# The end of a decoder layer: last block by column halves, last root on GpSimd, last scalings in one tile

## The chip, the cores and the metric

The kernel runs on one core of one Trainium2 chip. The metric is the device time of one execution in microseconds; the figure of a kernel is the median over several executions. The engines are named as in the profile: PE is TensorE (PEld its weight loads), DVE is VectorE, ACT is ScalarE, POOL is GpSimd, SP is SyncE, which issues most of the DMA transfers.

## What is computed

One layer of a decoder over 512 tokens of width 1024, all in float32. Only the last part matters here: the channel mixer's down projection, its residual add, and the final norm.

```python
        u2 = _rmsnorm(h, norm2_g[l])
        z = _causal_dwconv(u2 @ w_ffn_up[l], ffn_dw_w[l], ffn_dw_b[l])
        h = h + (jax.nn.silu(z[..., :FFN_DIM]) * z[..., FFN_DIM:]) @ w_ffn_down[l]
    return _rmsnorm(h, final_g)

def _rmsnorm(x, g):
    xf = x.astype(jnp.float32)
    y = xf * lax.rsqrt(jnp.mean(xf * xf, axis=-1, keepdims=True) + EPS)
    return (y * g.astype(jnp.float32)).astype(x.dtype)
```

## The kernel before

Tokens lie in four row tiles t = 0 to 3 of P = 128 tokens, the width of 1024 in two halves n = 0, 1 of T = 512 columns. The residual is held in SBUF as eight tiles `hres[t, n]` of 128x512. Each float32 operand is split into a high and a low part, and one product of such operands is three matmuls (`mm3`, lines 288 to 294: low x high, high x low, high x high). A PSUM tile is 128x512 float32.

The two big square projections (output and down projection) run through `seven` (line 816), which forms a two-by-two block product from seven block products instead of eight. The steps go in the order of `STEPS`: a11, a12, s1, n2, s4, n3, a22. Each step has two blocks, i = 0 and 1, and a block is four operand pairs by three matmuls, twelve matmuls of 512 columns into one PSUM tile (line 844). After a block, line 859 adds or subtracts the PSUM tile into one `hres` tile on VectorE; `into` says which. The step a12 completes `hres` of row tiles 0 and 1, n = 0; s4 completes row tiles 0 and 1, n = 1; n3 completes row tiles 2 and 3, n = 1; a22, the last step, completes row tiles 2 and 3, n = 0. So the last block of the program is (a22, i = 1), which completes row tile 3.

The down projection is done in three groups of channels; in the last of them `complete` is `last_complete` (line 995) and `at` is `last_at` (line 1001). When a half of a row tile is complete, `Finish.half` squares it on ScalarE with a running sum (`square_sum`, line 875: an activation and the reading of its accumulator) and multiplies it by the gain on VectorE (line 976), in place for the first half found, into a `tmp` tile for the second. When both halves are there, `total_rstd` adds the two sums and EPS on VectorE (line 880), and `rsqrt` raises the total to the power -1/2 on GpSimd (line 340). `Finish.store` scales both halves by that root: the half found last on ScalarE (line 985), the other on ScalarE (line 990) for row tiles 0 and 1, on VectorE (line 988) for 2 and 3; each half goes out by its own DMA of 256 KB that SyncE issues (lines 986 and 991).

Weights of the last step come in through the two buffers `kept` (lines 184 to 204): they are split into high and low parts by ScalarE (line 231) and VectorE (line 232) one step ahead. The tile framework orders the instructions of each engine when the program is built, by when it expects them to be ready, so the order on an engine can differ from that of the text; waits between engines and on buffers are put in by it as well.

Of the kernel before, what the change touches and what calls it, by code (L numbers as in the profile page):

```python
# [10 lines left out]
F32 = mybir.dt.float32  # L11
# [3 lines left out]
AF = mybir.ActivationFunctionType  # L15
ALU = mybir.AluOpType

P = 128
D = 1024
T = 512  # L20
NT = T // P
# [10 lines left out]
EPS = 1e-6  # L32
# [32 lines left out]
def trunk_layer(ctx: ExitStack, tc: tile.TileContext, a: dict, out: bass.AP):  # L65
    nc = tc.nc
# [5 lines left out]
    def scoped(name, bufs, side="left"):  # L72
        scope = ExitStack()
        return scope, scope.enter_context(tc.tile_pool(name=name, bufs=bufs, side=side))
# [14 lines left out]
    def nm(s):  # L89
        return f"{s}_{next(names)}"  # L90

    def heap(dt=F32):
        return hp.tile([P, T], dt, tag="h", name=nm("h"))

    def tmp(n=T):
        return tp.tile([P, n], F32, tag="tmp", name=nm("tmp"), bufs=5)
# [7 lines left out]
    def small(n, tag):  # L104
        return tp.tile([P, n], F32, tag=tag, name=nm(tag), bufs=4)

    def mm_bank():
        return ps.tile([P, T], F32, tag="mm", name=nm("mm"), bufs=5)

    def ax_bank():  # L110
        return ps.tile([P, T], F32, tag="ax", name=nm("ax"), bufs=3)
# [7 lines left out]
    mhalf = cp.tile([P, NT], F32, name="mhalf")  # L119
# [36 lines left out]
    kept = {}  # L156
# [97 lines left out]
    def prefetch(n):  # L254

        while len(ready) < min(used[0] + n, len(order)):
            split_weight()

    def weight(name, j, ahead=LOOK):
        assert order[used[0]] == (name, j)  # L260
        prefetch(1)
        used[0] += 1
        prefetch(ahead)
        fill(RATE)
        return ready[used[0] - 1]
# [6 lines left out]
    def fill(n):  # L272
        room[0] += n
        while chains and room[0] > 0:
            room[1] += 1
            chain = chains[room[1] % min(2, len(chains))]
            share, work = chain.pop(0)
            room[0] -= share
            with tc.issue_after(pace[0].ins):
                work()  # L280
            if not chain:
                chains.remove(chain)
                if not chains and after:
                    chains.append(after.pop()())
        if not chains:
            room[0] = 0.0
# [51 lines left out]
    def rsqrt(v, n):  # L338
        r = small(n, "rstd")
        nc.gpsimd.tensor_tensor(r, v, mhalf[:, :n], ALU.pow)  # L340
        return r
# [6 lines left out]
    def junk(n):  # L348
        return tp.tile([P, n], BF16, tag="junk", name=nm("junk"), bufs=1)
# [109 lines left out]
    for k in range(KT):  # L459
# [4 lines left out]
        c = heap()  # L464
# [95 lines left out]
    rows = slice(32, 32 + RANK)  # L560
# [9 lines left out]
    rows = slice(96, 96 + RANK)  # L570
# [184 lines left out]
    late_scope, late = scoped("late", 1, "right")  # L755


    part = [None] * KT
# [15 lines left out]
    H = T // 2  # L774
# [18 lines left out]
    for p, q in O_PAIRS:  # L793
# [6 lines left out]
        s1, n2, n3, s4 = e1[:, :H], e1[:, H:], e2[:, :H], e2[:, H:]  # L800
# [12 lines left out]
    ctx.push(res_scope)  # L813


    def seven(name, pairs, acts, complete, at=lambda step, i: None):

        bank = {"x": [mm_bank(), mm_bank()], "y": [mm_bank(), mm_bank()], "z": [ax_bank(), ax_bank()]}
        of = {"a11": "x", "n2": "x", "n3": "x", "a22": "x", "s1": "y", "s4": "y", "a12": "z"}

        into = {
            "a11": (0, 0, ALU.add, False),
            "a12": (0, 0, ALU.add, True),
            "s1": (1, 1, ALU.add, False),
            "n2": (0, 1, ALU.subtract, False),
            "s4": (0, 1, ALU.add, True),  # L830
            "n3": (1, 1, ALU.subtract, True),
            "a22": (1, 0, ALU.add, True),
        }

        def products(step, i, parts):
            acc = bank[of[step]][i]
            opens = step in ("a11", "s1", "a12")
            for d, w in parts:
                for j, pair in enumerate(acts[2 * d : 2 * d + 2]):
                    ah, al = (x[:, i * P : (i + 1) * P] for x in pair[step])  # L840
                    c = slice(j * T, (j + 1) * T)

                    read = 2 * d + j == len(acts) - 1
                    mm3(acc, (ah, al), (w[0][:, c], w[1][:, c]), opens and d == 0 and j == 0, read, not opens)

        steps = list(STEPS)
        while steps:
            step, d = steps.pop(0)
            parts = [(d, weight(name, (pairs, step, d)))]
            if steps and steps[0] == (step, 1):  # L850
                steps.pop(0)
                parts.append((1, weight(name, (pairs, step, 1))))
            for i in range(2):
                products(step, i, parts)
                if parts[-1][0] == 1:
                    at(step, i)
                    half, n, op, whole = into[step]
                    t = 2 * half + i
                    nc.vector.tensor_tensor(hres[t, n], hres[t, n], bank[of[step]][i], op)  # L859
                    if whole:  # L860
                        complete(t, n)


    gain2 = load_gain("norm2_g")
    hres = {}
# [6 lines left out]
    def square_sum(key, src, n):  # L872
        if key not in ss2:
            ss2[key] = small(2, "ss2")
        nc.scalar.activation(junk(T), src, AF.Square, scale=1.0 / 32.0, accum_out=ss2[key][:, n : n + 1])

    def total_rstd(key):
        v = small(1, "var")
        s = ss2[key]
        nc.vector.scalar_tensor_tensor(v, s[:, 0:1], EPS, s[:, 1:2], ALU.add, ALU.add)  # L880
        return rsqrt(v, 1)
# [7 lines left out]

    normed, roots = {}, {}  # L890

    def o_complete(t, n):
        square_sum(("n2", t), hres[t, n], n)
        if n == (0 if t > 1 else 1):
            roots[t] = total_rstd(("n2", t))
            if t > 1:
                normed[t] = norm2(t, roots[t])
# [19 lines left out]
    ffn_scope, fp = scoped("ffn", 1)  # L917
    gain3 = load_gain("final_g")
# [31 lines left out]
    def second_of_pair(i, accs, w, acts):  # L950
# [11 lines left out]
        acts["s1"], acts["n2"], acts["s4"] = y(0), y(1), y(2)  # L962
        return acts

    class Finish:


        def __init__(self, t):
            self.t, self.found = t, []

        def half(self, n):
            hn = hres[self.t, n]
            square_sum(("n3", self.t), hn, len(self.found))
            g = gain3[:, n * T : (n + 1) * T]
            y = tmp() if self.found else hn
            nc.vector.tensor_tensor(y, hn, g, ALU.mult)
            self.found.append((n, y))

        def scale(self):
            self.r = total_rstd(("n3", self.t))  # L980

        def store(self, late):
            rows = slice(self.t * P, (self.t + 1) * P)
            (m, x), (n, y) = self.found
            nc.scalar.activation(y, y, AF.Copy, scale=self.r)
            nc.sync.dma_start(out[rows, n * T : (n + 1) * T], y)
            if late:
                nc.vector.tensor_scalar(x, x, self.r, None, ALU.mult)
            else:
                nc.scalar.activation(x, x, AF.Copy, scale=self.r)  # L990
            nc.sync.dma_start(out[rows, m * T : (m + 1) * T], x)

    ends = [Finish(t) for t in range(NT)]

    def last_complete(t, n):
        ends[t].half(n)
        if len(ends[t].found) == 2 and t > 1:
            ends[t].scale()
            ends[t].store(True)

    def last_at(step, i):

        if (step, i) == ("a22", 0):
            for end in ends[:2]:
                end.scale()
            for end in ends[:2]:
                end.store(False)

    for gi, pairs in enumerate(GROUPS):
        acts = []  # L1010
        early = {}
        if gi == 0:

            ws = [weight("w_up", j, 0) for i in pairs[0] for j in (i, FT + i)]
            accs = [mm_bank() for _ in ws]
            for lo in (0, T // 2):
                for j, (w, acc) in enumerate(zip(ws, accs)):
                    col_tile(w, acts2, acc, lo, lo + T // 2)
                    if lo == 0 and j > 1:
                        to_channels(normed[j], u2, j)  # L1020
            early = {pairs[0][0]: accs[:2], pairs[0][1]: accs[2:]}

        def both(i):
            return early.get(i) or [col_tile(weight("w_up", i), acts2), col_tile(weight("w_up", FT + i), acts2)]

        for p, q in pairs:
            w, found = first_of_pair(p, both(p))
            acts.append(second_of_pair(q, both(q), w, found))
        if gi < len(GROUPS) - 1:
            seven("w_down", pairs, acts, lambda t, n: None)  # L1030
        else:
            seven("w_down", pairs, acts, last_complete, last_at)
    ffn_scope.close()


# [87 lines left out]
```

## Time and profile before

| what | value |
|---|---|
| median of 3 executions | 849.79 us (849.37 to 850.01) |
| the profiled execution: its time | 850.15 us |
| the profiled execution: its span | 848.4 us |
| mean granted clock of TensorE | 0.998 |
| TensorE busy | 835.3 us, 98% |
| matmuls of 128x512 (line 292 in the large groups) | 384 ns mean, pipelined |

The span is the time from the first to the last instruction in the trace; the execution's own time has 1.75 us more around it. Rows of the time line give the start in us from the span's start, the duration in us, the engine, the line, the operation, out<-in with the program's names and shapes, and in square brackets how long the engine was idle before and what released it. Rows of groups give the busy time in us and the mean of one in ns, then the idle time before. Matmuls overlap in the pipeline: each row of a matmul of 512 columns says 0.39 us, and they start about 0.23 us apart.

### The profile page before, as it was taken

The numbers are of one execution on the slowest core, as the hardware profiler recorded it, in microseconds if no ns is written. First come the engines' busy times: TensorE is split into PE (matmuls) and PEld (weight loads), VectorE is DVE, ScalarE is ACT, GpSimd is POOL, SyncE is SP. The second block draws the span as 40 slices with busy tenths as digits, with TensorE's granted clock in tenths as the row PEclk, the third lists the DMA queues.
The fourth block names the chain that finished last, engine by engine and source line by source line (L and its number), as shares of the span: only waits on it lengthen the run. The fifth ranks groups of instructions, "written<-read, shape, count | busy, mean of one in ns | idle before, by whom it ended". The sixth has DMA issues, their size and how long they took to land.

```text
span 848.4 us, 9947 instructions
## 1 busy us (share of the span) xinstructions
PE 835.3 (98%) x3814; PEld 691.0 (81%) x3814; DVE 646.1 (76%) x913; ACT 383.3 (45%) x531; POOL 42.6 (5%) x60
## 2 busy tenths in 40 slices
PE   8999999999999999999999999999999999999996
PEld 6888888888888888788888788888888888888885
DVE  5479879999998788744688749778767777677795
ACT  5433336535443422449444526444334443444454
POOL 1000000000100100000001100000100010000011
PEclk9999999999999999999999999999999999999999
DMA  8223232222222322222338533225732238222462
GB/s 288 94 100 104 95 107 81 97 96 81 94 75 75 124 100 99 75 99 75 119 82 228 191 124 126 100 81 118 211 126 99 71 89 273 96 94 98 100 124 101
DMA packets 28579, 97.79 MB, mean 115 GB/s; under 512 B 3233, under 2 KB 3361, under 8 KB 28530
## 3 DMA queue, kind: packets, MB, share of 16 engines
q1 hardware_dynamic: 25074, 85.35, 28.8%
q0 software_dynamic: 3456, 11.80, 7.8%
q8 instruction: 30, 0.49, 0.2%
q14 instruction: 19, 0.16, 0.1%
HBM read 95.03 MB, written 2.10 MB: 114 GB/s over the span
## 4 chain that ended last, share of the span: by engine, by line
PE 96%; DVE 1%; DMA 1%; ACT 1%; issue 0%; POOL 0%; SPq 0%; POOLq 0%; ACTq 0%
PE mm L292 30%; PE mm L293 29%; PE mm L294 29%; PE ax L293 1%; PE ax L294 1%; PE ax L292 1%; PE ax L698 1%; DMA raw<-in_w_v_dram 1%; PE ax L680 1%; PE ax L700 1%; DVE hres L859 0%; PE ax L369 0%; PE ax L667 0%; PE ax L715 0%; PE ax L666 0%
## 5 line engine op out<-in xcount | busy, mean ns | idle before, releaser
L292 PE MATMUL mm<-uh,wlo 128*128 128x512 f32 (+1 forms) x768 | 294.4, 384 | 1.2 <-DVE wlo L250 0.6
L293 PE MATMUL mm<-ul,whi 128*128 128x512 f32 (+1 forms) x768 | 292.0, 381 | 0.2 <-DVE ul L374 0.2
L294 PE MATMUL mm<-uh,whi 128*128 128x512 f32 (+1 forms) x768 | 292.2, 381 | 0.0
L247 ACT CAST whi<-raw 128x1024 fp32r<-128x1024 f32 x116 | 120.8, 1045 | 134.6 <-PE mm L294 101.3
L250 DVE TENSOR_TENSOR wlo<-raw,whi 128x1024 fp32r<-128x1024 f32 x116 | 141.0, 1219 | 38.3 <-ACT whi L247 37.8
L292 PEld LDWEIGHTS mm<-uh,wlo 128*128 128x128 f32 x768 | 144.2, 188 | 29.0 <-ACT uh L373 1.0
L293 PEld LDWEIGHTS mm<-ul,whi 128*128 128x128 f32 x768 | 144.5, 188 | 27.8 <-DVE ul L374 0.6
L294 PEld LDWEIGHTS mm<-uh,whi 128*128 128x128 f32 x768 | 144.4, 188 | 27.9
L457 DVE SCALAR_TENSOR_TENSOR c<-h,pp,c 128x511 f32<-128x511 f32 (+14 forms) x240 | 162.3, 728 | 0.7
L925 DVE SCALAR_TENSOR_TENSOR tmp<-mm,pp,tmp 128x511 f32<-128x511 f32 x88 | 65.8, 748 | 66.0 <-ACT tmp L923 64.8
L923 ACT ACTIVATE tmp<-mm,pp 128x512 f32<-128x512 f32 x44 | 34.3, 780 | 62.9 <-PE mm L294 62.9
L231 ACT CAST whi<-kept 128x1024 fp32r<-128x1024 f32 (+1 forms) x32 | 31.6, 992 | 24.4 <-DVE kept L211 12.8
L232 DVE TENSOR_TENSOR wlo<-kept,whi 128x1024 fp32r<-128x1024 f32 (+1 forms) x32 | 36.6, 1152 | 2.8 <-ACT whi L231 2.8
L859 DVE TENSOR_TENSOR hres<-hres,mm 128x512 f32<-128x512 f32 x48 | 32.6, 682 | 5.6 <-PE mm L294 3.8
L231 ACT CAST whi<-raw 128x1024 fp32r<-128x1024 f32 (+1 forms) x24 | 23.6, 992 | 19.8 <-PE mm L294 19.5
L340 POOL TENSOR_TENSOR rstd<-var,mhalf 128x1 f32<-128x1 f32 (+1 forms) x20 | 17.6, 884 | 262.2 <-DVE var L705 195.6
L232 DVE TENSOR_TENSOR wlo<-raw,whi 128x1024 fp32r<-128x1024 f32 (+1 forms) x24 | 27.3, 1152 | 3.5 <-ACT whi L231 3.5
L292 PE MATMUL mm<-whi,ul 128*128 128x512 f32 x64 | 26.3, 411 | 1.3 <-DVE ul L374 1.3
L293 PE MATMUL mm<-wlo,sh 128*128 128x512 f32 x66 | 26.0, 395 | 0.0
L294 PE MATMUL mm<-whi,sh 128*128 128x512 f32 x66 | 26.0, 394 | 0.0
L292 PE MATMUL mm<-whi,sl 128*128 128x512 f32 x66 | 25.9, 394 | 0.0
L292 PE MATMUL mm<-h,wlo 128*128 128x512 f32 x64 | 25.7, 402 | 0.0
(220 smaller groups left out, 1124.4 us busy)
## 6 DMA issues: line engine op xcount, KB each, us to landing
raw<-in_w_up_dram SPq DMA_DIRECT2D x44, 512.0 KB, 3.3
raw<-in_w_glu_dram SPq DMA_DIRECT2D x16, 512.0 KB, 3.6
raw<-in_w_down_dram SPq DMA_DIRECT2D x15, 512.0 KB, 3.2
kept<-in_w_down_dram POOLq DMA_DIRECT2D x10, 512.0 KB, 5.1
raw<-in_w_v_dram SPq DMA_DIRECT2D x8, 512.0 KB, 3.9
raw<-in_w_qk_dram SPq DMA_DIRECT2D x8, 512.0 KB, 3.2
raw<-in_w_r_dram SPq DMA_DIRECT2D x8, 512.0 KB, 3.3
raw<-in_w_gb_dram SPq DMA_DIRECT2D x8, 512.0 KB, 3.3
```

Source lines behind the costliest of these rows:

```text
L231: nc.scalar.copy(hi, raw)
L232: nc.vector.tensor_tensor(lo, raw, hi.bitcast(F32), ALU.subtract)
L247: nc.scalar.copy(hi, raw)
L250: pace[0] = nc.vector.tensor_tensor(lo, raw, hi.bitcast(F32), ALU.subtract)
L292: nc.tensor.matmul(acc, ll, rh, start=first, stop=False, **kw)
L293: nc.tensor.matmul(acc, lh, rl, start=False, stop=False, **kw)
L294: nc.tensor.matmul(acc, lh, rh, start=False, stop=last, **kw)
L340: nc.gpsimd.tensor_tensor(r, v, mhalf[:, :n], ALU.pow)
L457: nc.vector.scalar_tensor_tensor(y[:, s:], c[:, : T - s], w, y[:, s:], ALU.mult, ALU.add)
L859: nc.vector.tensor_tensor(hres[t, n], hres[t, n], bank[of[step]][i], op)
L923: nc.scalar.activation(z, acc, AF.Identity, bias=pp[:, PP_FB + m : PP_FB + m + 1], scale=w[2])
L925: nc.vector.scalar_tensor_tensor(z[:, s:], acc[:, : T - s], w[j], z[:, s:], ALU.mult, ALU.add)
```

## The change

- `seven` gets a parameter `fine`. Where it is set, which is in the last group of the down projection, the block (a22, i = 1) is done in two pieces of 256 columns: all products of the first piece, its add into `hres`, its completion, then the same for the second.
- `products` takes the columns `lo:hi` of the PSUM tile and of the weights.
- `Finish` takes parts of any width: `part(n, c)` squares the part on ScalarE, multiplies it by the gain, and keeps a running sum of the squares' sums on VectorE, the first with EPS, all but the last part.
- `scale` adds the last part's sum and takes the power, both on GpSimd.
- For row tiles 2 and 3 the gain products go into one tile of 128x1024 (a buffer of `kept`) instead of two. `store` scales its first 384 columns on ScalarE and the other 640 on VectorE, each with its own DMA.
- Row tiles 0 and 1 are stored as before, with the sum now on GpSimd.

```diff
-    def seven(name, pairs, acts, complete, at=lambda step, i: None):
+    def seven(name, pairs, acts, complete, at=lambda step, i: None, fine=False):
...
-        def products(step, i, parts):
-            acc = bank[of[step]][i]
+        def products(step, i, parts, lo=0, hi=T):
+            acc = bank[of[step]][i][:, lo:hi]
...
-                    c = slice(j * T, (j + 1) * T)
+                    c = slice(j * T + lo, j * T + hi)
...
+            half, n, op, whole = into[step]
             for i in range(2):
-                products(step, i, parts)
-                if parts[-1][0] == 1:
-                    at(step, i)
-                    half, n, op, whole = into[step]
-                    t = 2 * half + i
-                    nc.vector.tensor_tensor(hres[t, n], hres[t, n], bank[of[step]][i], op)
-                    if whole:
-                        complete(t, n)
+                t = 2 * half + i
+                pieces = [(0, H), (H, T)] if fine and step == "a22" and i == 1 else [(0, T)]
+                for lo, hi in pieces:
+                    products(step, i, parts, lo, hi)
+                    if parts[-1][0] == 1:
+                        at(step, i)
+                        c = slice(lo, hi)
+                        nc.vector.tensor_tensor(hres[t, n][:, c], hres[t, n][:, c], bank[of[step]][i][:, c], op)
+                        if whole:
+                            complete(t, n, c)
...
+    SPLIT = 5 * P
+
     class Finish:
         def __init__(self, t):
-            self.t, self.found = t, []
-
-        def half(self, n):
-            hn = hres[self.t, n]
-            square_sum(("n3", self.t), hn, len(self.found))
-            g = gain3[:, n * T : (n + 1) * T]
-            y = tmp() if self.found else hn
-            nc.vector.tensor_tensor(y, hn, g, ALU.mult)
-            self.found.append((n, y))
+            self.t, self.width = t, 0
+            self.y = fp.tile([P, D], F32, tag="kept", name=nm("y"), bufs=2) if t > 1 else None
+            self.ss = small(4, "ss4")
+            self.parts = []
+
+        def part(self, n, c):
+            hn = hres[self.t, n][:, c]
+            k = len(self.parts)
+            nc.scalar.activation(junk(T)[:, c], hn, AF.Square, scale=1.0 / 32.0, accum_out=self.ss[:, k : k + 1])
+            y = self.y[:, n * T + c.start : n * T + c.stop] if self.y else tmp() if self.parts else hn
+            nc.vector.tensor_tensor(y, hn, gain3[:, n * T + c.start : n * T + c.stop], ALU.mult)
+            self.parts.append((n, y))
+            self.width += c.stop - c.start
+            if k == 0:
+                self.sum = small(1, "var")
+                nc.vector.tensor_scalar(self.sum, self.ss[:, 0:1], EPS, None, ALU.add)
+            elif self.width < D:
+                nc.vector.tensor_tensor(self.sum, self.sum, self.ss[:, k : k + 1], ALU.add)
 
         def scale(self):
-            self.r = total_rstd(("n3", self.t))
+            k = len(self.parts) - 1
+            self.r = small(1, "rstd")
+            nc.gpsimd.tensor_tensor(self.sum, self.ss[:, k : k + 1], self.sum, ALU.add)
+            nc.gpsimd.tensor_tensor(self.r, self.sum, mhalf[:, :1], ALU.pow)
 
-        def store(self, late):
+        def store(self):
             rows = slice(self.t * P, (self.t + 1) * P)
-            (m, x), (n, y) = self.found
-            nc.scalar.activation(y, y, AF.Copy, scale=self.r)
-            nc.sync.dma_start(out[rows, n * T : (n + 1) * T], y)
-            if late:
-                nc.vector.tensor_scalar(x, x, self.r, None, ALU.mult)
-            else:
-                nc.scalar.activation(x, x, AF.Copy, scale=self.r)
-            nc.sync.dma_start(out[rows, m * T : (m + 1) * T], x)
+            if self.y:
+                lo, hi = self.y[:, : D - SPLIT], self.y[:, D - SPLIT :]
+                nc.scalar.activation(lo, lo, AF.Copy, scale=self.r)
+                nc.sync.dma_start(out[rows, : D - SPLIT], lo)
+                nc.vector.tensor_scalar(hi, hi, self.r, None, ALU.mult)
+                nc.sync.dma_start(out[rows, D - SPLIT :], hi)
+                return
+            for n, y in reversed(self.parts):
+                nc.scalar.activation(y, y, AF.Copy, scale=self.r)
+                nc.sync.dma_start(out[rows, n * T : (n + 1) * T], y)
...
-            seven("w_down", pairs, acts, last_complete, last_at)
+            seven("w_down", pairs, acts, last_complete, last_at, True)
```

## The prediction, made before the changed kernel was run

> **What bounds the kernel now.** I read the page first (busy time by engine, then the chain that ended last), then the time line of the last 15 us, then rows of other stages that show pieces which the change brings in.
>
> ```profile
> PE 835.3 (98%) x3814; PEld 691.0 (81%) x3814; DVE 646.1 (76%) x913; ACT 383.3 (45%) x531; POOL 42.6 (5%) x60
> ...
> PE 96%; DVE 1%; DMA 1%; ACT 1%; issue 0%; POOL 0%; SPq 0%; POOLq 0%; ACTq 0%
> ```
>
> TensorE sets the time up to its last product, and everything the change touches lies around that product. The time line of the end (start, duration, engine, line):
>
> ```profile
> 838.32 0.40 PE L294 MATMUL mm<-whi,ah 128*128 128x512 f32 x1
> 838.55 0.39 PE L292 MATMUL mm<-whi,al 128*128 128x512 f32 x1
> 838.75 0.69 DVE L859 TENSOR_TENSOR hres<-hres,mm 128x512 f32<-128x512 f32 x1 [0.56 <-PE mm L294]
> 839.47 0.69 DVE L976 TENSOR_TENSOR tmp<-hres,gain 128x512 f32<-128x512 f32 x1
> 840.07 0.19 ACT L875 ACTIVATION_READ_ACCUMULATOR junk<-hres 128x1 f32 x1
> 840.60 0.55 POOL L340 TENSOR_TENSOR rstd<-var,mhalf 128x1 f32<-128x1 f32 x1 [5.60 <-DVE var L880]
> 841.10 0.39 PE L294 MATMUL mm<-whi,ah 128*128 128x512 f32 x1
> 841.18 0.48 DVE L988 TENSOR_SCALAR hres<-hres,rstd 128x512 f32<-128x512 f32 x1 [0.73 <-POOL rstd L340]
> 841.58 0.68 DVE L859 TENSOR_TENSOR hres<-hres,mm 128x512 f32<-128x512 f32 x1
> 842.36 0.63 ACT L875 ACTIVATE junk<-hres 128x512 bf16<-128x512 f32 x1 [0.45 <-DVE hres L859]
> 842.89 0.19 ACT L875 ACTIVATION_READ_ACCUMULATOR junk<-hres 128x1 f32 x1
> 843.11 0.16 DVE L880 SCALAR_TENSOR_TENSOR var<-ss 128x1 f32<-128x1 f32 x1
> 843.41 0.55 POOL L340 TENSOR_TENSOR rstd<-var,mhalf 128x1 f32<-128x1 f32 x1 [2.27 <-DVE var L880]
> 844.00 0.72 ACT L985 ACTIVATE tmp<-tmp,rstd 128x512 f32<-128x512 f32 x1 [0.92 <-POOL rstd L340]
> 844.00 0.48 DVE L988 TENSOR_SCALAR hres<-hres,rstd 128x512 f32<-128x512 f32 x1 [0.73 <-POOL rstd L340]
> 844.51 0.33 SPq L991 DMA_DIRECT2D out_dram<-hres  x1
> 844.96 0.36 SPq L986 DMA_DIRECT2D out_dram<-tmp  x1
> ```
>
> The last block (a22, i = 1, row tile 3) starts at 838.55 and its last product ends at 841.10 + 0.39 = 841.49: 2.94 us. Behind it runs one chain: add (841.58 to 842.26), square and its sum (842.36 to 843.08), the sum of the two halves on VectorE, the power on GpSimd (843.41 to 843.96), two scalings from 844.00, two stores. Row tile 2 runs the same chain 2.8 us earlier, beside the products.
>
> **The last block by halves (the first part).** Twelve products of 512 columns become 24 of 256, each with its own weight load.
>
> ```profile
> 489.65 1.22 DVE L250 TENSOR_TENSOR wlo<-raw,whi 128x1024 fp32r<-128x1024 f32 x1
> 490.92 0.39 PE L292 MATMUL mm<-uh,wlo 128*128 128x256 f32 x1 [0.62 <-DVE wlo L250]
> ...
> 492.22 0.28 PE L292 MATMUL mm<-uh,wlo 128*128 128x256 f32 x1
> ...
> 493.29 0.28 PE L292 MATMUL mm<-uh,wlo 128*128 128x256 f32 x1
> ```
>
> From 492.22 to 493.29 nine products of 256 columns start: 0.119 us each, weight loads included, and one ends 0.28 after its start. So 24 without a stop take 23 x 0.119 + 0.28 = 3.02 us, 0.08 more than 2.94. The first two rows give the way from VectorE to TensorE: 490.87 to 490.92, 0.05 us.
>
> But both halves lie in one PSUM tile, and the add of the first half stands before the products of the second in the text. No row shows a product waiting for the reader of the other half. The nearest case is in the gated attention, where two products fill the halves of one tile and ScalarE squares each half:
>
> ```profile
> 282.28 0.59 PE L700 MATMUL ax<-state,q 128*128 128x256 f32 x2
> ...
> 283.14 0.59 PE L700 MATMUL ax<-state,q 128*128 128x256 f32 x2
> 283.84 0.38 ACT L703 ACTIVATE junk<-ax 128x256 bf16<-128x256 f32 x1 [0.74 <-PE ax L700]
> ```
>
> The first half was full at 282.28 + 0.59 = 282.87, and its square did not start before the second was too (283.73): reader and writer of different halves are kept apart there. I take it that this holds here in the other direction. Then the first half ends at 838.55 + 11 x 0.119 + 0.28 = 840.14; VectorE is free at 839.47 + 0.69 = 840.16 and adds 256 columns. Its cost and ScalarE's:
>
> ```profile
> L956 DVE TENSOR_TENSOR v<-w,f 128x256 f32<-128x256 f32 x11 | 4.7, 423 | 0.2
> L703 ACT ACTIVATE junk<-ax 128x256 bf16<-128x256 f32 x16 | 6.2, 384 | 3.5 <-PE ax L700 3.3
> L231 ACT CAST whi<-raw 128x1024 fp32r<-128x1024 f32 x21 | 22.0, 1046 | 18.0 <-PE mm L294 17.7 <-ACT whi L231 0.3
> L938 ACT CAST yh<-w 128x512 fp32r<-128x512 f32 x11 | 6.8, 620 | 28.7 <-DVE w L946 28.7
> ```
>
> 0.42 for the add brings 840.59, TensorE goes on at 840.64 and ends at 840.64 + 1.31 + 0.28 = 842.23: 0.74 later than before. Queued behind the waiting product is only the rest of the block, and only this chain waits for it. (The product after a wait shows 0.39 and not 0.28, so up to 0.11 more.) The Trainium skill, "PSUM — Partial Sum Buffer", section "PSUM bank collisions raise a hardware error", speaks against the edit: TensorE writing and VectorE reading one bank collide whichever columns they touch, and have to be held apart by bank. With that rule the sum keeps its 0.66 us of stop, without it only 0.08 is lost; no run here shows a collision.
>
> What the halves give back: the add starts 0.03 after the products (838.32 + 0.40 to 838.75) and not 0.09, since row tile 2's scaling no longer stands in front of it (-0.06); it takes 0.42 and not 0.68 (-0.26); the square of 256 columns costs 0.384 in L703 and by the slope of the casts (1.046 - 0.620 over 512 columns, 0.83 ns each) 0.21 less than 0.63: I take -0.23. The first half's own square, gain product and small sum lie under the second half's products (840.64 to 842.23), some 0.5 us of each engine.
>
> **Sum and power on GpSimd.** From the square's end to the power were 843.41 - 843.08 = 0.33 us, through VectorE. Now: the way to GpSimd (0.14, 843.27 to 843.41), an addition of one column, a way from GpSimd to itself, the power as before.
>
> ```profile
> 0.94 0.10 POOL L380 MEMSET mhalf<- 128x4 f32 x1
> ...
> 7.14 0.30 POOL L133 TENSOR_SCALAR_AFFINE_SELECT tmp<-tmp 128x128 f32<-128x128 f32 x1
> 7.51 0.29 POOL L136 CAST keep<-tmp 128x128 uint8<-128x128 f32 x1
> ```
>
> L136 reads what L133 wrote and starts 0.07 after it. The trace has no addition on GpSimd: it costs between 0.10 (a memset) and 0.55 (the same instruction form with a power in it). I take 0.15, nearer the memset, because 128 columns of a select or cast cost only 0.3, so most of the 0.55 is the power. Sum 0.14 + 0.15 + 0.07 = 0.36: +0.03, with ends -0.02 and +0.43. The Trainium skill, "GPSIMD Engine Reference", section 3.1, gives 4497 ns for an addition of 2048 columns at about 2.6 cycles each; an estimate from that page leaves about 0.06 us fixed, by which this part would be -0.06 and the whole sum 0.09 lower. For row tiles 0 and 1 the same two operations lie under products. Row tile 2's root comes at 841.2 (840.26 + 0.14 + 0.15 + 0.07 + 0.55, and 0.03 to the reader) and its two scalings end by 841.8, ahead of the last add at 842.26; a root 0.5 later would eat that cover. VectorE loses four sums of 0.16 and gets as many small ones.
>
> **The last scalings and stores.** ScalarE scales 384 columns: 0.72 - 128 x 0.83 ns = 0.61. VectorE scales 640: 0.48 + 128 columns, between nothing and 128 x (0.69 - 0.42)/256 = 0.13; I take 0.55. Now the stores:
>
> ```profile
> GB/s 253 0 0 0 0 0 0 0 0 0 0 0 0 0 0 0 194 365 417 365 365 194 37 0 0 0 97 395 380 365 387 283 0 0 0 30 0 0 0 0
> ...
> out_dram<-hres SPq DMA_DIRECT2D x2, 256.0 KB, 2.0
> out_dram<-tmp SPq DMA_DIRECT2D x2, 256.0 KB, 2.2
> ```
>
> In this view of 838 to 849 us each slice is 0.275 us: the last two stores move their 512 KB back to back at some 380 GB/s from 845.2 on. SyncE issued the first 0.03 after VectorE's scaling, the second 0.45 later, although ScalarE had been done since 844.72. So ScalarE's 0.11 is worth nothing; what counts is when the first store goes out, 0.48 + 0.03 before and 0.55 + 0.03 after: +0.07. Ends: +0.13 if ScalarE's store goes first, -0.15 if only the last landing counts and shrinks from 256 to 192 KB (64 KB at 380 GB/s, 0.17, less a little issue). The gain products of tiles 2 and 3 go to a buffer that the last weights used; those were split by VectorE itself before, so nothing waits.
>
> **The sum.** +0.74 - 0.06 - 0.26 - 0.23 + 0.03 + 0.07 = +0.29 us. The profiled execution took 850.15 (span 848.4, 1.75 around it), so it would take 850.44; it lies 0.36 above the median of 849.79, against which the forecast is 850.1. With the ends of each term (restart 0 to +0.11, GpSimd -0.05 to +0.40, stores -0.22 to +0.06 beside the values taken) it runs from +0.0 to +0.9, and the three runs before spread by 0.64: 849.4 to 850.9 is the range of this case alone.
>
> **Rivals.**
>
> 1. *No wait between the halves* (they are told apart by column). TensorE ends at 841.57. Row tile 2's 640-column scaling then holds VectorE from 841.2 to 841.75: the last add starts 0.18 after the products and not 0.09. 0.08 + 0.09 - 0.26 - 0.23 + 0.03 + 0.07 = -0.22, so 849.6; -0.37 if the add goes first. For it: the halves share no byte. Against it: the row at 283.84. Chance 0.08.
>
> 2. *Row tile 2's scaling stands ahead of the first half's add on VectorE.* The order of each queue is fixed when the program is built, and it is not that of the text: the store of L991 goes out before that of L986. Then VectorE waits for tile 2's root until 841.2, scales until 841.75, adds the first half until 842.17, and TensorE, which waits for that add, goes on at 842.22 and not 840.64: +1.58 on top of +0.29, 851.7, slower by 0.22%. It decides as soon as the root is expected before the end of the first half's products. For it, such an order exists in the output projection:
>
> ```profile
> 474.48 0.39 PE L294 MATMUL mm<-whi,sums 128*128 128x512 f32 x1
> 474.64 1.41 DVE L887 SCALAR_TENSOR_TENSOR un<-hres,rstd,gain 128x512 f32<-128x512 f32 x2 [0.76 <-POOL rstd L340]
> 475.97 0.68 DVE L859 TENSOR_TENSOR hres<-hres,mm 128x512 f32<-128x512 f32 x1
> ```
>
> The block was done at 474.87, but its add waited behind two operations that hung on a root. Against it: there the root was ready 0.23 us earlier; here it is ready 1.06 us after the half (840.14). Chance 0.10.
>
> 3. *Something outside the end moves*, because the queues are ordered anew or buffers shift. The end itself cannot give 0.2%: between the last product and the first store lie 844.51 - 841.49 = 3.0 us, of which the power, a scaling and the ways stay. Chance 0.10, most of it within half a microsecond.
>
> **Chances.** The forecast has 0.72. A difference under 0.2% (1.7 us) is about what a measurement of this kernel cannot tell from none. Within it lie the forecast, rival 1, a fifth of rival 2 and a small part of rival 3: 0.83. Slower takes the rest of rival 2 and half of rival 3: 0.13. Faster can come from rival 3 alone: 0.04. The range for 8 in 10 goes from rival 1's far end (849.3) to rival 2 (851.7).
>
> **What will show it.** The last 24 products in two groups, with a gap of about 0.78 us between starts where an add of 256 columns fits in; the last product ending near 842.2; a GpSimd pair of about 0.15 and 0.55 in place of VectorE's sum; the scalings from about 844.2; SyncE's stores 0.45 apart. Twenty-four starts without a gap show rival 1, a scaling of 640 columns ahead of the first 256-column add shows rival 2. A time under 849.3, or a difference ahead of 838.5 us, makes the prediction wrong.

## The result and the profile after

| | before | changed |
|---|---|---|
| median of 6 executions each, same chip | 849.59 us (848.75 to 850.01) | 846.02 us (845.47 to 847.18) |
| ratio of the two | | 0.996 (0.9948 to 0.9973) |
| the profiled execution: its time, its span | 850.15, 848.45 us | 846.52, 844.80 us |
| last block starts | 838.55 us | 834.37 us |
| from there to the end of the span | 9.90 us | 10.43 us |

The changed kernel is faster by 0.4%. The end became 0.53 us longer; what comes ahead of it became 4.18 us shorter. -4.18 + 0.53 = -3.65, the difference of the two spans. The spans here are read from the trace to the hundredth. The profile's views round them to 848.4 and 844.8, and with the rounded ones the end before seems to take 9.85 us and its growth to be 0.58: the expectation for the experiment with the whole last block uses these two figures. For the same reason the 1.75 us around the span of the kernel before are 1.70.

The page of the changed kernel, busy times and shares of the chain:

```profile
PE 832.0 (98%) x3826; PEld 691.4 (82%) x3826; DVE 646.2 (76%) x916; ACT 383.1 (45%) x533; POOL 42.5 (5%) x64
...
PE 96%; DVE 1%; ACT 1%; DMA 1%; issue 1%; POOL 0%; POOLq 0%; ACTq 0%
```

Twelve products more, as the diff says, yet TensorE is busy for 3.3 us less. The other engines' sums moved by a tenth or two. So nearly all of the gain lies in the products themselves: what the span has beside TensorE's busy time went only from 13.1 to 12.8 us. Where does it begin? The time lines of both kernels show one and the same product, no. 1312 of the run, in the projections of the gated attention, an earlier stage of the same layer. Before:

```profile
290.41 0.39 PE L294 MATMUL mm<-h,whi 128*128 128x512 f32 x1
```

Changed, that product and the first of the last block:

```profile
289.96 0.40 PE L294 MATMUL mm<-h,whi 128*128 128x512 f32 x1
...
834.37 0.28 PE L292 MATMUL mm<-whi,al 128*128 128x256 f32 x1
```

Up to there 0.45 us came in, of which more below. From there to the last block the kernel before took 838.55 - 290.41 = 548.14 us and the changed one 834.37 - 289.96 = 544.41: 3.73 less. Each product has two operands in SBUF: a loaded one of 128x128, which a weight load brings in ahead of it, and a streamed one of 128x512. The groups of matmuls over the whole run (line, operands as `out<-streamed,loaded`, count | busy us, mean ns of one | idle before) show which products changed. Before:

```profile
L294 PE MATMUL mm<-uh,whi 128*128 128x512 f32 x704 | 274.3, 390 | 0.0
L294 PE MATMUL mm<-whi,sh 128*128 128x512 f32 x66 | 26.0, 394 | 0.0
L294 PE MATMUL mm<-h,whi 128*128 128x512 f32 x64 | 25.3, 395 | 0.0
L294 PE MATMUL mm<-ch,whi 128*128 128x512 f32 x64 | 25.0, 391 | 0.0
```

Changed:

```profile
L294 PE MATMUL mm<-uh,whi 128*128 128x512 f32 x704 | 274.2, 390 | 0.0
L294 PE MATMUL mm<-whi,sh 128*128 128x512 f32 x66 | 25.7, 389 | 0.0
L294 PE MATMUL mm<-ch,whi 128*128 128x512 f32 x64 | 25.3, 395 | 0.0
L294 PE MATMUL mm<-h,whi 128*128 128x512 f32 x64 | 24.9, 390 | 0.0
```

The large group, with the operand `u`, stands still. The down projection (`whi,sh`) and the gates (`h,whi`) gained 5 ns a product, the convolution's projection (`ch,whi`) lost 4. Idle time is 0.0 in all of them. One product follows the other every 227 ns or every 232, and what counts is that step. Two products of the down projection, 21 steps apart, from the time line before and after:

```profile
802.29 0.40 PE L292 MATMUL mm<-whi,yl 128*128 128x512 f32 x1
...
807.17 0.40 PE L292 MATMUL mm<-whi,yl 128*128 128x512 f32 x1
```

```profile
799.01 0.39 PE L292 MATMUL mm<-whi,yl 128*128 128x512 f32 x1
...
803.77 0.39 PE L292 MATMUL mm<-whi,yl 128*128 128x512 f32 x1
```

4.88/21 = 232.4 ns before, 4.76/21 = 226.7 ns after. By stage, from the starts of the same products in both traces (product numbers count all matmuls in order):

```text
products            what                               before    changed   difference, us
1312-1610           gated attention, gates and out     69.25     68.03     -1.22
1610-1990           convolution's projection           85.21     85.40     +0.19
1990-2170           output projection                  41.75     41.44     -0.31
2680-2850           down projection, group 1           39.49     38.53     -0.96
3140-3260           down projection, group 2           27.89     27.41     -0.48
3640-last block     down projection, group 3           37.63     36.72     -0.91
all others          (up projection above all)                              -0.04
```

What could change the speed of products that no line of the diff touches? The change has a new small buffer, `self.ss = small(4, "ss4")`: four buffers of 32 bytes in each partition, ahead of everything that is allocated later in that part of SBUF. The addresses in the built program show that the buffers of the heap, of the convolution and of the feed-forward part moved by 128 bytes; those of `ch` and `hres` stayed where they were. Place within 256 bytes:

```text
operand                                               before    changed
weights whi, wlo                                        64        64
u (up projection, and most of the run), sums            64        64
h, a, s, y (gates, output and down projections), c     192        64
ch (high parts of the convolution)                     224       224
```

Where the streamed and the loaded operand of a product lie at the same place within 256 bytes, the step is 227 ns; 128 bytes apart it is 232. That is the theory which the experiments test.

Now the end, from the time line of the changed kernel:

```profile
835.69 0.28 PE L294 MATMUL mm<-whi,ah 128*128 128x256 f32 x1
836.00 0.42 DVE L863 TENSOR_TENSOR hres<-hres,mm 128x256 f32<-128x256 f32 x1
836.48 0.39 PE L292 MATMUL mm<-whi,al 128*128 128x256 f32 x1 [0.51 <-DVE hres L863]
836.70 0.28 PE L293 MATMUL mm<-wlo,ah 128*128 128x256 f32 x1
837.01 0.62 ACT L1005 ACTIVATE y<-y,rstd 128x384 f32<-128x384 f32 x1 [0.93 <-POOL rstd L999]
837.01 0.55 DVE L1007 TENSOR_SCALAR y<-y,rstd 128x640 f32<-128x640 f32 x1 [0.58 <-POOL rstd L999]
837.53 0.40 ACT L983 ACTIVATE junk<-hres 128x256 bf16<-128x256 f32 x1
837.90 0.28 PE L294 MATMUL mm<-whi,ah 128*128 128x256 f32 x1
838.05 0.16 DVE L992 TENSOR_TENSOR var<-var,ss 128x1 f32<-128x1 f32 x1 [0.16 <-ACT junk L983]
838.22 0.42 DVE L863 TENSOR_TENSOR hres<-hres,mm 128x256 f32<-128x256 f32 x1
838.73 0.42 ACT L983 ACTIVATE junk<-hres 128x256 bf16<-128x256 f32 x1 [0.71 <-DVE hres L863]
839.05 0.19 ACT L983 ACTIVATION_READ_ACCUMULATOR junk<-hres 128x1 f32 x1
839.32 0.19 POOL L998 TENSOR_TENSOR var<-ss,var 128x1 f32<-128x1 f32 x1 [2.35 <-ACT junk L983]
839.58 0.55 POOL L999 TENSOR_TENSOR rstd<-var,mhalf 128x1 f32<-128x1 f32 x1
840.17 0.62 ACT L1005 ACTIVATE y<-y,rstd 128x384 f32<-128x384 f32 x1 [0.93 <-POOL rstd L999]
840.17 0.55 DVE L1007 TENSOR_SCALAR y<-y,rstd 128x640 f32<-128x640 f32 x1 [1.07 <-POOL rstd L999]
840.75 0.33 SPq L1008 DMA_DIRECT2D out_dram<-y  x1
841.20 0.36 SPq L1006 DMA_DIRECT2D out_dram<-y  x1
```

The reader is to see the stop: the first half is full at 835.69 + 0.28, its add runs from 836.00 to 836.42, and the next product starts at 836.48 with 0.51 us idle, released by that add. And a near miss: ScalarE puts tile 2's scaling (837.01) ahead of the first half's square (837.53), so VectorE's small sum (838.05 to 838.21) is done 0.01 ahead of the last add, which starts 0.04 after the products' end (838.18).

### The profile page after: what moved, and what is told of

It is laid out like the page before. It is cut to its first block, busy times and chain, and to the rows that moved or that the text cites. A ratio compares the mean times of both kernels' runs of the same rounds, so it can differ in the third digit from the quotient of the medians.

```text
span 844.8 us, 9983 instructions
## 1 busy us (share of the span) xinstructions
PE 832.0 (98%) x3826; PEld 691.4 (82%) x3826; DVE 646.2 (76%) x916; ACT 383.1 (45%) x533; POOL 42.5 (5%) x64
## 4 chain that ended last, share of the span: by engine, by line
PE 96%; DVE 1%; ACT 1%; DMA 1%; issue 1%; POOL 0%; POOLq 0%; ACTq 0%
PE mm L293 29%; PE mm L292 29%; PE mm L294 29%; PE ax L698 1%; PE ax L294 1%; PE ax L293 1%; PE ax L292 1%; PE ax L680 1%; PE ax L700 1%; PE ax L369 1%; PE mm L398 0%; DVE hres L863 0%; PE ax L667 0%; PE ax L715 0%; PE ax L666 0%
## 5 line engine op out<-in xcount | busy, mean ns | idle before, releaser
L863 DVE TENSOR_TENSOR hres<-hres,mm 128x512 f32<-128x512 f32 (+1 forms) x49 | 32.8, 672 | 4.2 <-PE mm L294 2.9
L340 POOL TENSOR_TENSOR rstd<-var,mhalf 128x1 f32<-128x1 f32 (+1 forms) x16 | 14.1, 890 | 241.5 <-DVE var L705 196.7
L293 PE MATMUL mm<-wlo,uh 128*128 128x512 f32 x64 | 25.8, 404 | 0.0
L294 PE MATMUL mm<-whi,uh 128*128 128x512 f32 x64 | 25.7, 401 | 0.0
```

The lines of the kernel that those rows point to most:

```text
L293: nc.tensor.matmul(acc, lh, rl, start=False, stop=False, **kw)
L294: nc.tensor.matmul(acc, lh, rh, start=False, stop=last, **kw)
L863: nc.vector.tensor_tensor(hres[t, n][:, c], hres[t, n][:, c], bank[of[step]][i][:, c], op)
```

## The experiments

**The shift alone.** The kernel before, and in it one line more: it allocates 128 bytes that nothing reads ahead of the buffers that moved, and writes the first number of each partition:

```diff
+        nc.gpsimd.memset(tp.tile([P, 32], F32, tag="pad", name=nm("pad"), bufs=1)[:, :1], 0.0)
```

> The kernel before, with one unused 128-byte buffer ahead of the heap, so that heap, convolution and feed-forward buffers lie 128 bytes further on, as in the changed kernel; nothing of the change. Theory A (the gain comes from where the buffers lie): the products of the down projections start 0.227 us apart and not 0.232, and the time is 3.4 to 4.3 us under the kernel before, 845.3 to 846.2. Theory B (the gain comes from the edits): within 0.5 us of the kernel before, spacing 0.232.

Measured: 850.05 us against 853.6 for the kernel before on that chip, ratio 0.9961 (0.994 to 0.9982), within the interval of the change itself. From product 1312 to the last block: 544.41 us, to the hundredth what the changed kernel takes. The time line of the down projection, 21 steps:

```profile
803.13 0.39 PE L293 MATMUL mm<-whi,yl 128*128 128x512 f32 x1
...
807.89 0.39 PE L293 MATMUL mm<-whi,yl 128*128 128x512 f32 x1
```

226.7 ns. A kernel with none of the change's code has all of its gain.

**The change without the shift.** The small sums use an existing tag instead of a new one:

```diff
-            self.ss = small(4, "ss4")
+            self.ss = small(4, "ss2")
```

> The whole change, but the sums of squares use the small buffers that were there already, so that no buffer moves. Theory A: only the end differs, 0.3 to 0.9 us slower than the kernel before, 849.9 to 850.5, spacing 0.232. Theory B: about 846.0, spacing 0.227.

Measured: 852.83 us against 853.6, ratio 0.9997 (0.9977 to 1.0017), and from product 1312 to the last block:

```profile
290.91 0.39 PE L294 MATMUL mm<-h,whi 128*128 128x512 f32 x1
...
839.07 0.28 PE L292 MATMUL mm<-whi,al 128*128 128x256 f32 x1
```

548.16 us, where the kernel before takes 548.14. From there to the end it takes 10.40 us, as the changed kernel does (10.43). With the first experiment this settles where the gain is from: all of it from 128 bytes, none from what the change does.

**Place or distance?** 128 bytes ahead of everything, the weights too:

```diff
+    pad = cp.tile([P, 32], F32, name="pad")
+    nc.gpsimd.memset(pad[:, :1], 0.0)
```

> The kernel before with the 128 bytes put ahead of the weights, so that weights, activations and heap all move and keep their distance to each other. A1 (the distance between the two operands of a product counts): as the kernel before, within 0.7 us. A2 (each operand's own place within 256 bytes counts, 64 good, 192 bad): the products of the up projection, now at 192, slow down from 0.227 to about 0.232, some 2100 of them, and the time is 8 to 13 us above the kernel before. Theory B: as the kernel before.

Measured: 851.85 us against 853.6, ratio 0.9999 (0.9977 to 1.0021); 548.13 us. (The medians differ by 1.75 us, but that chip's times for the kernel before spread from 850.11 to 856.1; the interval holds no difference as well as 0.2% either way.) 18 steps of the down projection:

```profile
808.20 0.40 PE L294 MATMUL mm<-whi,yl 128*128 128x512 f32 x1
...
812.39 0.39 PE L294 MATMUL mm<-whi,yl 128*128 128x512 f32 x1
```

4.19/18 = 232.8 ns, though `y` now lies where the first experiment put it. The up projection kept its 227 with its operands at another place. So what counts is the distance between the two operands, and not the place of either.

**What distances?** The padding of the first experiment in other sizes, one profiled execution each. 64 bytes:

> The kernel before with heap, convolution and feed-forward buffers 64 bytes further on (at 0 within 256 bytes, weights stay at 64). A with a period of 128 bytes or more: spacing of the down projection stays at about 0.232 and the time is near 849.6. A with a period of 64 bytes: 0.232 too, since the distance is unchanged by it. Only if the good places are wider than one point: 0.227, near 845.8.

384 bytes (128 + 256):

> The kernel before with 384 bytes ahead of the heap: the same place within 256 bytes as with 128. If the pattern repeats every 256 bytes, the products of the down projection come 0.227 apart; if it repeats every 512 or more, not 0.227.

256 bytes:

> The kernel before with 256 bytes ahead of the heap. If the pattern repeats every 256 bytes: 0.232 as before. If the good places are elsewhere: another spacing.

160 bytes, which leaves the operands 32 bytes apart:

> The kernel before with 160 bytes ahead of the heap: 32 bytes past the good place (96 within 256 bytes, weights at 64). If only the equal place is good: 0.232, or between as with 64 bytes. If a neighbourhood is good: 0.227.

Measured, in this order: 853.17, 847.5, 849.13 and 851.09 us. The times alone say little at this spread, the steps do: mean time from one start to the next in ns, over all recorded products of a pair (streamed,loaded), worked out from the traces:

```text
                    bytes apart   whi,sh   wlo,sh   whi,yl   h,whi    product 1312 to last block, us
before                  128       232.2    232.2    233.2    232.8    548.14
+128 (alone)              0       226.7    227.1    226.5    226.9    544.41
+128, weights too       128       232.4    232.4    232.6    233.1    548.13
+64                      64       226.9    232.2    228.6    233.2    546.6
+384                      0       226.7    226.7    226.9    227.4    544.37
+256                    128       232.1    232.6    232.8    232.8    548.14
+160                     32       233.3    233.2    233.2    233.3    548.69
changed                   0       226.2    227.2    226.9    227.0    544.41
```

384 is as good as 128 and 256 as bad as nothing: over the distances tried, the step repeats every 256 bytes. The 256 also show that neither the added line nor a move as such is worth anything. 32 bytes off is as bad as 128. At 64 bytes none of the outcomes expected came: some pairs take 227, others 229, 232 or 233, and no rule found here says which. The slow gates (`h,whi`) and the mixed down projection differ in which operand lies lower: there the streamed one by 64 bytes, here the loaded one. The time line with 160 bytes, 21 steps of 232.9 ns:

```profile
803.10 0.39 PE L293 MATMUL mm<-whi,yl 128*128 128x512 f32 x1
...
807.99 0.40 PE L293 MATMUL mm<-whi,yl 128*128 128x512 f32 x1
```

**The convolution's projection as well.** Its high parts `ch` lie at 224 in both kernels. The shift put its low parts at 64, and its three kinds of product went from 231.7 (`ch,wlo`), 231.7 (`c,whi`) and 230.1 ns (`ch,whi`) to 230.1, 233.2 and 233.3: the +0.19 us in the table by stage, -1.6 + 1.5 + 3.2 = 3.1 ns by 64 products each. That `c,whi` is slow although both lie at 64 shows that a pair isn't judged by itself when its neighbours in the sequence lie elsewhere. So the kernel before got both the 128 bytes and 160 bytes behind the first `ch`, which brings the others to 64 as well:

```diff
+        if k == 0:
+            nc.gpsimd.memset(late.tile([P, 40], F32, tag="pad2", name=nm("pad"), bufs=1)[:, :1], 0.0)
         ca[k] = split(s, hi, ctile(F32R))
```

> The kernel before with two unused buffers: 128 bytes ahead of the heap as in the first run, and 160 bytes beside the convolution's high parts, so that these too lie at 64 within 256 bytes, as the weights do. If the distance between a product's two operands counts, the 192 products of the convolution's projection come 0.227 apart and not 0.230 to 0.233, 0.9 to 1.1 us less than with the first buffer alone: 4.5 to 5.5 us under the kernel before (ratio 0.9935 to 0.9947). If not, as with the first buffer alone, ratio 0.995 to 0.9965.

Measured: 845.52 us (844.67 to 846.91) against 849.5, ratio 0.9951 (0.9939 to 0.9964). All three kinds of product take 226 to 227 ns. The time line has the two marks:

```profile
290.31 0.40 PE L295 MATMUL mm<-h,whi 128*128 128x512 f32 x1
...
833.62 0.39 PE L293 MATMUL mm<-whi,al 128*128 128x512 f32 x1
```

543.31 us between them, 1.10 less than with the 128 bytes alone, at the upper edge of what was expected. The ratio expected was 0.9935 to 0.9947, so 0.9951 misses it, and the interval reaches it only at its lower end: the end of this execution took 3.79 us from the issue of the second of the last two stores on, where the other kernels with the old end took 3.46 to 3.49. The next kernel, the other one with the 160 bytes, has 3.87 where the new end otherwise has 3.59 to 3.61, which speaks against chance. In both the extra lies in the second store alone: it lands 2.58 and 2.64 us after its issue (2.24 before, 2.35 changed), the first one 2.02 and 2.17 as in the kernels without the 160 bytes. Why, is open.

**Both in the changed kernel.** The 160 bytes alone are added to it, since its new small buffer does the rest.

> The changed kernel with the 160 bytes beside the convolution's high parts: all buffers that products read lie at 64 within 256 bytes. From the product with number 1312 to the start of the last block: 548.1 us before, 544.4 changed; 543.2 to 543.5 here. Whole time 0.8 to 1.2 us under the changed kernel's, ratio to the kernel before 0.9935 to 0.9955.

Measured: 845.73 us (845.14 to 847.14) against 849.67, ratio 0.9946 (0.9925 to 0.9966), and 543.33 us between the marks: both as expected. The whole time is 1.2 us under the changed kernel's by the two ratios; the profiled spans (844.23 against 844.80) differ by only 0.57, as 0.26 of the 1.08 gained are lost again behind the last stores' issue and 0.25 in the first 290 us. It beats the kernel before. Against the one with the old end (845.52 us, ratio 0.9951) the times can't tell which is better. From the start of the last block to the issue of the first of the last two stores the old end takes 5.97 us and the new one 6.37.

**What the end's parts cost.** Three experiments, all in the changed kernel. The last block whole, with the rest of the change (`fine` is False):

```diff
-            seven("w_down", pairs, acts, last_complete, last_at, True)
+            seven("w_down", pairs, acts, last_complete, last_at, False)
```

> The changed kernel with the last block in one piece; the sum on GpSimd, the one tile and its uneven shares stay. From the start of the last block to the end of the span: 9.85 us before, 10.43 changed. If the halves cost what the sum says (stop 0.66, restart 0.11, slower weight loads 0.08, less 0.55 given back), 10.0 to 10.2. If the other two parts cost the 0.58, 10.4. The whole time 0.2 to 0.5 us under the changed kernel's in the first case.

Measured: 846.7 us against 849.5, ratio 0.9963 (0.995 to 0.9977), and 10.45 us from the last block on, no shorter than with the halves (10.43). That is the outcome expected if the other two parts cost all of it, but its time line has something new:

```profile
838.09 0.55 DVE L1007 TENSOR_SCALAR y<-y,rstd 128x640 f32<-128x640 f32 x1 [1.02 <-POOL rstd L999]
838.56 0.68 DVE L863 TENSOR_TENSOR hres<-hres,mm 128x512 f32<-128x512 f32 x1
...
839.61 0.63 ACT L983 ACTIVATE junk<-hres 128x512 bf16<-128x512 f32 x1 [0.91 <-DVE hres L863]
```

The add ends at 839.24, and the square starts 0.37 later; in the kernel before the same pair is 0.10 apart (841.58 + 0.68 to 842.36). The chain of waits calls 0.32 of it "issue", time in which ScalarE waited for nothing that the profile shows. Without this gap of 0.27 the end would take 10.18, and the halves would cost 0.25; with it they cost nothing. What the gap is, one execution doesn't say, and the price of the halves stays open between the two. The first row shows a second cost of the whole block: VectorE is on tile 2's scaling of 640 columns until 838.64, and the add starts 0.22 behind the last product (838.34) and not 0.10 as before.

All 24 products ahead of both adds:

```diff
                 for lo, hi in pieces:
                     products(step, i, parts, lo, hi)
+                for lo, hi in pieces:
                     if parts[-1][0] == 1:
```

> The changed kernel with all 24 products of the last block ahead of both adds. If the second half's products waited for the add of the first (0.51 us idle and a slow start in the changed kernel), the block takes 3.0 us and not 3.81, with no gap, and the end from the block's start 10.0 to 10.4 and not 10.43. If the gap has another cause it stays.

Measured: 846.95 us in one execution. The time line around the middle and the end of the block:

```profile
836.02 0.28 PE L294 MATMUL mm<-whi,ah 128*128 128x256 f32 x1
836.14 0.28 PE L292 MATMUL mm<-whi,al 128*128 128x256 f32 x1
...
837.46 0.28 PE L294 MATMUL mm<-whi,ah 128*128 128x256 f32 x1
837.81 0.75 DVE L864 TENSOR_TENSOR hres<-hres,mm 128x256 f32<-128x256 f32 x2
...
839.14 0.42 ACT L984 ACTIVATE junk<-hres 128x256 bf16<-128x256 f32 x1
```

The halves follow each other without a gap, and the block takes 3.03 us (3.02 in the prediction, for a block without a stop) and not 3.81: the stop in the changed kernel is the wait for the first half's add, and 24 products without it take 0.10 more than the twelve of the kernel before (2.94), 0.15 more than the twelve of the experiment above (2.88), whose operands lie at the same place. From the block's start to the end it takes 10.50 us, outside the 10.0 to 10.4 expected and no shorter than with the stop: what TensorE saves comes back behind it, as two adds (0.75 in all) and two squares, the second of which starts only at 839.14.

The last sum on VectorE:

```diff
-            nc.gpsimd.tensor_tensor(self.sum, self.ss[:, k : k + 1], self.sum, ALU.add)
+            nc.vector.tensor_tensor(self.sum, self.ss[:, k : k + 1], self.sum, ALU.add)
```

> The changed kernel with the last sum of squares on VectorE again and the power on GpSimd. From the end of the square to the end of the power: 0.88 us before, 0.89 changed; 0.85 to 0.95 here if the place of the sum is worth nothing, under 0.75 or over 1.0 if it is worth something.

```profile
839.40 0.18 ACT L983 ACTIVATION_READ_ACCUMULATOR junk<-hres 128x1 f32 x1
839.62 0.16 DVE L998 TENSOR_TENSOR var<-ss,var 128x1 f32<-128x1 f32 x1 [0.17 <-ACT junk L983]
839.92 0.55 POOL L999 TENSOR_TENSOR rstd<-var,mhalf 128x1 f32<-128x1 f32 x1 [2.27 <-DVE var L998]
```

Measured: from the end of the square to the end of the power 839.58 to 840.47, 0.89 us; in the changed kernel 839.24 to 840.13, 0.89 too. The place of the sum is worth nothing: the way to GpSimd takes 0.08, its addition 0.19 and the way within it 0.07; the way to VectorE takes 0.04, its addition 0.16 and the way from it to GpSimd 0.14. The whole execution took 846.83 us.

## Why the prediction was wrong

The forecast was 850.1 us and no change; the kernel takes 846.0 and is faster by 0.4%, under its range of 849.3 to 851.7.

**The step that failed** is the sum's reach. "Everything the change touches lies around that product" was true of the instructions and not of the memory: the sum has no term for the new small buffer, so it was costed at nothing, and what it moved lies under 548 us of TensorE's work. Rival 3 named the mechanism ("buffers shift") but sized it "most of it within half a microsecond", with no price worked out from rows. It measured -3.73 us (548.14 to 544.41), and the shift alone gives all of it. The prediction's own last line, a difference ahead of 838.5 us, is what happened.

Could it have been seen? The rows were there: in the profile of before a product of the same shape takes 390 ns in one group (`uh,whi`) and 394 or 395 in others (`whi,sh`, `h,whi`), in one execution (mean granted clock 0.998) and with no idle time. These 5 ns on some 700 products (3.73 us by 5.4 ns each) are a loss in the kernel before that had no explanation; the forecast did not ask for one.

**The end, term by term.** The sum gave +0.29, and it measured +0.53 (9.90 to 10.43).

| term | predicted, us | measured, us | from |
|---|---|---|---|
| the block's products | +0.74 (up to +0.85) | +0.87 | 834.37 to 838.18 is 3.81; before 2.94 |
| start of the add | -0.06 | -0.06 | 0.04 behind the products; before 0.10 |
| the add | -0.26 | -0.26 | 0.42; before 0.68 |
| the square and its sum | -0.23 | -0.21 | 838.73 to 839.24 is 0.51; before 0.72 |
| sum on GpSimd | +0.03 | +0.01 | 0.34 to the power; before 0.33 |
| scaling, 640 columns | +0.07 | +0.07 | 0.55; before 0.48 |
| behind the second store's issue | 0 | +0.12 | 3.60; before 3.48 |

(The measured terms add up to 0.54; the 0.01 is rounding.) The mechanism at the end was right, and the +0.53 lies between the bounds of +0.0 and +0.9. The gap of 0.79 us between two starts (835.69 to 836.48) was predicted at 0.78, and the three gains behind it came within 0.02. Two sizes were off. The restart of TensorE costs 0.10 of the 0.13 that the block took more, which the prediction had in its bounds and not in its value: the first product after the gap takes 0.39, and the next starts 0.22 later instead of 0.12. And the last stores end 0.12 later behind their issue, although the second was issued 0.45 after the first as before. All five executions with the new end and no 160 bytes behind `ch` have 3.59 to 3.61 there, against 3.46 to 3.49 in the seven with the old end, so it belongs to the change; which part of it (the rows of 384 and 640 columns, or the tile that they come from) was not tried.

**PSUM.** The first half's add held the second half's products (0.51 us idle), and with the order of the text changed it did not. That is a wait which the program contains. The Trainium skill's rule ("PSUM — Partial Sum Buffer", "PSUM bank collisions raise a hardware error") is that TensorE's writes and another engine's reads of one bank have to be kept apart, whichever columns they touch; the row of 0.51 us idle agrees with it. What a collision would do, no run here shows.

**GpSimd's addition** took 0.19 us, above the 0.15 taken and three times the estimate of 0.06 from the Trainium skill's page "GPSIMD Engine Reference", section 3.1; the measurement decides. That the whole term came within 0.02 is luck in part: the way from ScalarE to GpSimd took 0.08 and not the 0.14 that the prediction carried over from VectorE, and the two errors nearly cancel.

**Rival 1**, no wait between the halves, fell with the gap. **Rival 2**, tile 2's scaling ahead of the first half's add on VectorE, didn't come: the add stands at 836.00 and the scaling at 837.01. But the same thing happened on ScalarE, where nobody looked for it. Tile 2's scaling went ahead of the first half's square and used up all of its cover: the small sum that hangs on it ends 0.01 us before the last add.

**Without the shift**, the change does what the forecast said, no difference that can be told from none: ratio 0.9997 (0.9977 to 1.0017). The interval is too wide to see the end's half microsecond; the time line shows it, 10.40 us against 9.90.

## What to carry to other kernels

An edit that adds, drops or resizes a buffer can move the buffers behind it, as four of 32 bytes did here with operands of stages far from the edit, so compare the addresses of both programs, and the time from one product to the next stage by stage, ahead of any reasoning about the edited place. A control that shifts the buffers and does nothing else tells the two apart in one run. And where products of one shape take 390 ns in one stage and 395 in another at the same clock, look at where their streamed and loaded operands lie: here the two at the same place within 256 bytes, over a whole sequence of products, gave 227 ns a step and not 232.

## What the runs showed of the hardware

- In a sequence of 128x512 products that all have the same distance between their two operands in SBUF, counted within 256 bytes, the time from one product to the next was 226 to 227 ns at 0, 232 to 233 at 32 and at 128, and mixed at 64 (227 to 233). It is the distance that counts, since moving both by 128 bytes left the down projection at 232 and the up projection at 227. In a mixed sequence a pair's own distance didn't decide: `c,whi` at distance 0 took 233.2 between products of `ch`, and 227 when `ch` lay there too. This is measured; why it is so is not shown.
- The steady part repeats closely: between the same two products six kernels with the down projection's operands at distance 0 and `ch` at 224 took 544.37 to 544.62 us, and four with distance 128 took 548.13 to 548.16. The start doesn't: product 1312 started at 290.41 us before, at 289.96 in the changed kernel, and at 294.08 in the first experiment.

```profile
294.08 0.40 PE L295 MATMUL mm<-h,whi 128*128 128x512 f32 x1
```

That is why the 0.45 us of the first 290 are not put down to the change, and why the stretch behind them tells kernels apart that a median of a few executions can't.
